# A Strassen-like projection on one Trainium2 core: smaller leading input chunks, a later place for the sums of squares, and a new order of pair one's products

## The chip, the cores and the metric

The kernel runs on one core of one Trainium2 chip. The time is device microseconds of one execution; runs of a kernel are repeated and their median is given. TensorE (PE) does the matrix products, VectorE (DVE) and ScalarE (ACT) the elementwise work, GpSimd (POOL) almost nothing, and SyncE (SP) issues nearly all DMA transfers. Each engine runs its own instructions in its own order and waits on semaphores for the others.

## What is computed

One layer of a decoder trunk for 1024 prompt tokens and 8 x 4 sample tokens, with the same weights, all in float32. Cut to what matters:

```python
h    = x * rsqrt(mean(x*x, -1) + EPS) * norm_g          # 1056 tokens x 1024
proj = h @ w_in                                          # 1024 -> 3072
b, c, u, z_a, v, z_b = split(proj)                       # six parts of 512
cu   = c * u
y_a  = b * conv3(cu) * silu(z_a)                         # three taps, causal
pooled = window_mean(v) - v                              # windows 2, 4, 8, 16 by channel group
y_b  = (pooled @ pool_w) * pool_scale * silu(z_b)
out  = rmsnorm(x + concat(y_a, y_b) @ w_out) * final_g
```

The last rows of `cu` and of `v` are returned as new states.

## The kernel before

**Precision and layout.** Channels lie on the 128 partitions and tokens along the free dimension. The 1056 tokens are three column groups n0, n1, n2 of 352. Each float32 operand is split into a high part in the matrix unit's reduced float32 (ACT writes it) and a low part, the rest (DVE writes it); `split2` does both. A product is the sum of three passes, high x low, low x high and high x high. A block of one weight tile, 128 x 512 of weights against 512 x 352 of x, is 12 matmuls (`block`, line 238).

**The first projection.** The norm gain multiplies x while it is split (`split_x`); the row scale 1/rms is applied later, to the products. The first pair of output tiles (v and z_b of group 0) is computed plainly by `project_first` (line 196), while the input arrives: for each of eight row tiles k of x, in the column groups n2 and n0, and then n1. The input comes in four leading chunks (`GROUPS`, line 109), in rows k = 0, then 1 and 2, then 3 and 4, then 5 to 7. A chunk is three loads on SP's queue: its part of the weights (`wfraw`) and its part of the columns n2 and n0 (`raw`). `prep_w0` and `split_x` split what has landed. The two loads of n1 follow.

**The other eleven pairs.** Each pair of output tiles (`PAIRS`) uses a scheme with fewer products: n0 and n1 and the two halves of the 1024 channels form a 2 x 2 block matrix of x, multiplied with the pair's 2 x 2 weight blocks in seven products; n2 is done plainly (`plain`, `plain1`: `l` and `r`, in pair one `lr`). The sums of x blocks are S1 to S4, the sums of weight blocks T1 to T4. A pair's weights are loaded as `wraw`, their differences are formed by `make_t` in `tw` (three DVE operations), and `make_unit` splits them into four units: a (B11, B21), b (B12, B22), c (T1, T3), d (T2, T4). Products add up in three PSUM banks a, b, c: B11 opens bank a, which is copied to s1 and then takes B21; bank b takes T2 and is read with s1 into t1, takes T3 and is read into t2, takes T4; bank c takes T1, is read with t2, takes B22. A bank must be read before the next product goes into it, since the partial sum is what is wanted.

**Pair one** is written out by hand (lines 536 to 588), since S1 to S4 are formed during it: S1f to S4f are float32 sums in the buffers of `raw`, and S1 and S4 overwrite `raw[1]` and `raw[0]`. From line 489 to 588 PE, ACT, DVE and POOL keep the order of the program (`manual_schedule`); from line 641 on only PE does, and the scheduler places the other engines' work, and may place work of both sections between one another. SP's queue is placed by the scheduler too. The PE order of pair one before is `lr0`, a: B11, `lr1`, a: B21, b: T2, c: T1, b: T3, b: T4, c: B22.

**The row scales** need the sums of squares of all tokens. Tokens 0 to 639 come by rows (`load_rows` of `xres`, `square_rows` on ACT with an accumulated sum): rows 0, 1 and 2 lie in the buffers of R, R2 and `up`, rows 3 and 4 in `x34`, a weight slot. The other tokens come from `raw` (`squares_head`, `squares_last`), are added on DVE into `acc` (`sums_last`, `sums_head`), and eight matmuls with one column each (`sums_rest`, line 285, tile `rest`) add over the partitions. `rows` turns all sums into 1/rms and builds a diagonal matrix of it (`diag`); `rows_out` spreads it by matmuls (`pr`) into R and then squares it into R2. In pair two these are the hooks `rest` and `rows`.

**Afterwards** the gates, the convolution and the pooling are done beside the products of later pairs, and the output projection (lines 684 and 756) ends the kernel.

Of the kernel before, what the change touches and what calls it, by code (L numbers as in the profile page):

```python
# [7 lines left out]
F32 = mybir.dt.float32  # L8
# [5 lines left out]
P = 128  # L14
D = 1024
# [47 lines left out]
def trunk(ctx, tc, xt, xres, xct, w_first, w_in, w_out, pool_w, par, fg, sconv, spool,  # L63
# [20 lines left out]
    def snap(name):  # L84
        return sp.tile([P, TN], F32, tag="snap", name=name)

    def bank(name):
        return ps.tile([P, 512], F32, tag="ps", name=name)
# [17 lines left out]
        nc.sync.dma_start(raw[n][:, k:k + m, :], xt[:, n * KD + k:n * KD + k + m, :])  # L106


    GROUPS = ((0, 1), (1, 2), (3, 2), (5, 3))
    for k, m in GROUPS:  # L110
        nc.sync.dma_start(wfraw[:, k:k + m, :], w_first[:, k:k + m, :])
        for n in (2, 0):
# [118 lines left out]
    def block(pt, p, w, x, first, last):  # L231

        u, i = WHERE[w]
        t = unit[p, u]
        seq = [(k, a, b) for k in range(KH) for a, b in ((0, 1), (1, 0))]
        seq += [(k, 0, 0) for k in range(KH)]
        for s, (k, a, b) in enumerate(seq):
            nc.tensor.matmul(pt, t[:, a, i, k * P:(k + 1) * P], x[:, b, k],  # L238
                             start=first and s == 0, stop=last and s == len(seq) - 1,
                             skip_group_check=True)  # L240
# [174 lines left out]

    def strassen(p, S1, S2, S3, S4, hooks):
        (q, j), (_, _) = PAIRS[p]
        if q == "v":  # L420
            left = vb[:, PM:]
            right = szb[j] = tmp(f"szb_{j}")
            scale = R
        elif q == "c":
            left, right = tmp(f"t_{j}"), tmp(f"um_{j}")
            scale = R2
        else:
            left, right = tmp(f"z_{j}"), tmp(f"y_{j}")
            scale = R

        def plain(i, name):
            pt = bank(name)[:, :TN]
            block(pt, p, ("B11", "B12")[i], pl[0], True, False)
            block(pt, p, ("B21", "B22")[i], pl[1], False, True)
            return pt

        a = bank(f"a_{p}")[:, :TN]
        s1 = snap(f"s1_{p}")
        block(a, p, "B11", A11, True, False)
        nc.scalar.copy(s1, a)  # L440
        b = bank(f"b_{p}")[:, :TN]
        block(b, p, "T2", S2, True, False)
        t1 = snap(f"t1_{p}")
        vt(t1, b, s1, op=ADD)
        c = bank(f"c_{p}")[:, :TN]
        block(c, p, "T1", S1, True, False)
        hooks.get("rest", lambda: None)()
        pL = plain(0, f"l_{p}")
        hooks.get("rows", lambda: None)()
        vt(left[:, n2], pL, scale[:, n2], op=MUL)  # L450
        block(a, p, "B21", A12, False, True)
        vt(left[:, n0], a, scale[:, n0], op=MUL)
        block(b, p, "T3", S3, False, False)
        t2 = snap(f"t2_{p}")
        vt(t2, b, s1, op=ADD)
        vt(right[:, n1], c, t2, op=ADD)
        hooks["early"]()
        pR = plain(1, f"r_{p}")
        if q == "v":
            vt(right[:, n2], pR, R[:, n2], op=MUL)  # L460
        elif q == "c":
            vt(up[:, 2 + 2 * TN:], pR, left[:, n2], op=MUL)
        else:
            nc.scalar.copy(right[:, n2], pR)
        hooks["middle"]()
        block(b, p, "T4", A22, False, True)
        vt(left[:, n1], b, s1, op=ADD)
        vt(left[:, n1], left[:, n1], scale[:, n1], op=MUL)
        block(c, p, "B22", S4, False, True)
        vt(right[:, n0], c, t1, op=ADD)  # L470
        hooks["late"]()

        if q == "v":
            after_v(j)
            vt(right[:, both], right[:, both], R[:, both], op=MUL)
            silu(right)
        elif q == "c":
            vt(up[:, 2:2 + 2 * TN], right[:, both], left[:, both], op=MUL)
            after_u(j)
        else:  # L480
            silu(left)
            vt(left, left, keep["yc"], op=MUL)
            vt(right, right, left, op=MUL)
            finish_mix(right, f"a_{j}")
# [4 lines left out]
    with tc.manual_schedule(engines={ET.PE, ET.Activation, ET.DVE, ET.Pool}):  # L489
        for k0, m in GROUPS:  # L490
            prep_w0(k0, m)
            for k in range(k0, k0 + m):
                for n in (2, 0):
                    split_x(n, k, wfraw[:, k, 2 * P:])
                    project_first(n, k)
        nc.vector.tensor_copy(gain.rearrange("p (k o) -> p k o", o=1), wfraw[:, :, 2 * P:])
        gk = [gain[:, k:k + 1] for k in range(KD)]
        load_w(1)
        nc.sync.dma_start(part, par)
        xk = [load_rows(t, q[:, :D]) for t, q in enumerate((R, R2, up[:, 2:]))]  # L500
        slot[1] = {"a": 2, "b": 3, "d": 4, "c": 0}
        slot[2] = {"a": 1, "d": 2, "c": 0, "b": 4, "spare": 3}
        acc = tmp("acc")
        for k in range(KD):
            split_x(1, k, gk[k])
            project_first(1, k)
        sh = squares_head(acc)

        S3f, S2f, S1f = raw[1][:, :KH], raw[1][:, KH:], raw[0][:, :KH]
        vt(S3f, raw[0][:, :KH], raw[1][:, :KH], op=SUB)  # L510
        make_unit(1, "a")
        for k in range(KH):
            nc.scalar.activation(S3f[:, k], S3f[:, k], AF.Copy, scale=gk[k])
        for k in range(KH):
            nc.vector.scalar_tensor_tensor(S2f[:, k], S2f[:, k], gk[KH + k], S3f[:, k], op0=MUL, op1=SUB)
        make_t(1)
        make_unit(1, "b")
        for i in range(2):
            nc.scalar.copy(heads[i][:, n2], pm[i, 2])
        sq = squares_last()  # L520
        make_unit(1, "d")
        S2 = xtile("xa", "S2")
        split(S2, S2f)
        S3 = xtile("xb", "S3")
        split(S3, S3f)
        make_unit(1, "c")
        x34 = wtile(1, [P, 2, D], "x34", F32)
        xk += [load_rows(t, x34[:, t - 3]) for t in (3, 4)]
        load_w(2)
        for k in range(KH):  # L530
            nc.vector.scalar_tensor_tensor(S1f[:, k], S1f[:, k], gk[k], S2f[:, k], op0=MUL, op1=ADD)
        for t in (3, 4, 2):
            square_rows(t, xk[t])


        t_0, um = tmp("t_0"), up[:, 2:]

        def plain1(i):
            pt = bank(f"lr{i}_1")[:, :TN]
            block(pt, 1, ("B11", "B12")[i], pl[0], True, False)  # L540
            block(pt, 1, ("B21", "B22")[i], pl[1], False, True)
            return pt

        pL = plain1(0)
        pa, pb, pc = (bank(f"{q}_1")[:, :TN] for q in "abc")
        s1, t1, t2 = (snap(f"{q}_1") for q in ("s1", "t1", "t2"))
        block(pa, 1, "B11", A11, True, False)
        nc.scalar.copy(s1, pa)
        pR = plain1(1)
        block(pa, 1, "B21", A12, False, True)  # L550
        S4f = [tp.tile([P, 2, TN], F32, tag="tmp", name=f"S4f_{h}") for h in range(2)]
        for k in range(KH):
            nc.vector.scalar_tensor_tensor(S4f[k // 2][:, k % 2], raw[0][:, KH + k], gk[KH + k], S2f[:, k],
                                           op0=MUL, op1=SUB)
        S1 = xtile("xc", "S1")
        split(S1, S1f)
        make_unit(2, "a")
        for n in (0, 1):
            for i in range(2):
                nc.scalar.copy(heads[i][:, cols[n]], pm[i, n])  # L560
        block(pb, 1, "T2", S2, True, False)
        vt(t1, pb, s1, op=ADD)
        S4 = xtile("xd", "S4")
        for h in range(2):
            ks = slice(2 * h, 2 * h + 2)
            split2(S4[:, 0, ks], S4[:, 1, ks], S4f[h])
        block(pc, 1, "T1", S1, True, False)
        nc.scalar.copy(t_0[:, n2], pL)
        make_t(2, (0,))
        nc.scalar.copy(t_0[:, n0], pa)  # L570
        block(pb, 1, "T3", S3, False, False)
        vt(t2, pb, s1, op=ADD)
        vt(um[:, n1], pc, t2, op=ADD)
        make_t(2, (1,))
        make_unit(2, "d")
        for t in range(2):
            square_rows(t, xk[t])
        block(pb, 1, "T4", A22, False, True)
        vt(t_0[:, n1], pb, s1, op=ADD)
        make_unit(2, "c")  # L580
        block(pc, 1, "B22", S4, False, True)
        vt(um[:, n0], pc, t1, op=ADD)
        for _ in sums_last(acc, sq):
            pass
        sums_head(acc, sh)
        make_unit(2, "b")
        vt(up[:, 2 + 2 * TN:], pR, t_0[:, n2], op=MUL)
        vt(up[:, 2:2 + 2 * TN], um[:, both], t_0[:, both], op=MUL)
# [267 lines left out]
```

## Time and profile before

| | us |
|---|---|
| median of 3 runs (lowest, highest) | 380.45 (379.07, 380.75) |
| the profiled execution | 380.98 |
| its span, from the first to the last instruction | 379.2 |
| PE busy in the span | 367.1 |
| DVE busy | 278.8 |
| ACT busy | 147.0 |

The mean granted TensorE clock of the span is 0.982. Times in rows of the profile are from the start of the span; L238 is line 238 of the kernel. A row of the timeline begins with start and duration, names the engine, the line, the operation, what is written and read and its shape, and ends with the idle time before it and what ended that idle time. A row of the waits has who waited for whom, the total, the number of times and the longest.

### The profile page before, as it was taken

Reading aid. Unit: us, or ns where it says so; the run is one execution under the profiler, and the core shown is the slowest. Engines: PE = TensorE matmul, PEld = TensorE weight load, DVE = VectorE, ACT = ScalarE, POOL = GpSimd, SP = SyncE. Lnnn points to the kernel's source line nnn. Section 1 sums busy time; section 2 is a strip of 40 time slices with the busy share of each in tenths; the row PEclk is TensorE's granted clock in tenths of the full one; section 3 lists DMA queues with packets and bytes.
Section 4 is the critical chain, followed back from the end, with each engine's and each line's share of the span. In section 5 each row is a group of like instructions: output and inputs, shape, how many; then the busy total and the mean of one; then the engine's idle time right before and its main releaser. Section 6 shows DMA issues by size and latency. Waiting matters only on the chain.

```text
span 379.2 us, 5200 instructions
## 1 busy us (share of the span) xinstructions
PE 367.1 (97%) x2114; PEld 353.4 (93%) x2114; DVE 278.8 (74%) x433; ACT 147.0 (39%) x231; POOL 1.4 (0%) x7
## 2 busy tenths in 40 slices
PE   6999997999999999999999999999999999999993
PEld 3999996999999999999999999999998889999883
DVE  3899869799999986769797666969269628222593
ACT  4899751863323323133332322332069215111212
POOL 0000000000000000000000000000000000000000
PEclk9899997899999999999999999999999999999998
DMA  7975002111131310303040130404639923100042
GB/s 226 394 258 190 34 0 67 73 33 80 57 112 58 112 57 19 150 2 111 0 169 0 54 137 11 165 3 129 270 110 349 417 89 124 45 0 2 0 180 111
DMA packets 13079, 41.67 MB, mean 110 GB/s; under 512 B 3712, under 2 KB 4224, under 8 KB 11648
## 3 DMA queue, kind: packets, MB, share of 16 engines
q1 hardware_dynamic: 12912, 41.02, 29.2%
q8 instruction: 16, 0.26, 0.3%
q10 hardware_dynamic: 144, 0.33, 0.2%
q14 instruction: 7, 0.06, 0.0%
HBM read 32.92 MB, written 8.42 MB: 109 GB/s over the span
## 4 chain that ended last, share of the span: by engine, by line
PE 93%; DVE 3%; DMA 2%; ACT 1%; SPq 0%; issue 0%; DVEq 0%
PE b L238 16%; PE po L686 15%; PE l L238 11%; PE a L238 11%; PE c L238 10%; PE r L238 10%; PE pc L756 10%; PE pm L196 6%; PE lr L238 2%; PE pp L392 2%; DMA raw<-in_xt_dram 2%; ACT R L249 1%; PE rest L285 0%; DVE wc L158 0%; DVE sq L274 0%; ACT wd L157 0%
## 5 line engine op out<-in xcount | busy, mean ns | idle before, releaser
L686 PE MATMUL po<-wo,mix 128*128 128x512 f32 (+1 forms) x264 | 56.5, 374 | 0.0
L686 PEld LDWEIGHTS po<-wo,mix 128*128 128x128 f32 x264 | 46.3, 188 | 9.7 <-DVE mix L158 0.2
L238 PE MATMUL a<-A,wa 128*128 128x352 f32 x264 | 46.4, 324 | 0.0
L238 PEld LDWEIGHTS a<-A,wa 128*128 128x128 f32 x264 | 43.3, 188 | 0.0
L238 PE MATMUL l<-pl,wa 128*128 128x352 f32 x240 | 42.5, 335 | 0.0
L238 PEld LDWEIGHTS l<-pl,wa 128*128 128x128 f32 x240 | 41.0, 197 | 0.0
L238 PE MATMUL r<-pl,wb 128*128 128x352 f32 x240 | 40.4, 324 | 0.0
L238 PEld LDWEIGHTS r<-pl,wb 128*128 128x128 f32 x240 | 39.1, 188 | 0.0
L756 PE MATMUL pc<-mix,wo 128*128 128x416 f32 x192 | 36.5, 351 | 0.0
L756 PEld LDWEIGHTS pc<-mix,wo 128*128 128x128 f32 x192 | 35.9, 188 | 0.5
L238 PE MATMUL c<-S,wc 128*128 128x352 f32 x132 | 23.4, 324 | 0.0
L238 PE MATMUL c<-S,wb 128*128 128x352 f32 x132 | 23.1, 324 | 0.0
L238 PE MATMUL b<-S,wc 128*128 128x352 f32 x132 | 23.1, 324 | 0.0
L238 PE MATMUL b<-S,wd 128*128 128x352 f32 x132 | 23.1, 324 | 0.0
L238 PE MATMUL b<-A,wd 128*128 128x352 f32 x132 | 23.1, 324 | 0.0
L157 ACT ACTIVATE wd<-tw 128x1024 fp32r<-128x1024 f32 x11 | 11.7, 1062 | 28.4 <-PE a L238 20.7
L238 PEld LDWEIGHTS c<-S,wc 128*128 128x128 f32 x132 | 21.6, 188 | 0.3 <-DVE wc L158 0.3
L238 PEld LDWEIGHTS b<-S,wc 128*128 128x128 f32 x132 | 21.7, 188 | 0.0
L238 PEld LDWEIGHTS c<-S,wb 128*128 128x128 f32 x132 | 21.7, 188 | 0.0
L238 PEld LDWEIGHTS b<-S,wd 128*128 128x128 f32 x132 | 21.7, 188 | 0.0
L238 PEld LDWEIGHTS b<-A,wd 128*128 128x128 f32 x132 | 21.7, 188 | 0.0
L758 DVE TENSOR_TENSOR zc<-pc,zc 128x416 f32<-128x416 f32 x8 | 4.7, 591 | 18.6 <-PE pc L756 18.6
(198 smaller groups left out, 530.7 us busy)
## 6 DMA issues: line engine op xcount, KB each, us to landing
wraw<-in_w_in_dram SPq DMA_DIRECT2D x11, 1024.0 KB, 4.7
woraw<-in_w_out_dram SPq DMA_DIRECT2D x8, 512.0 KB, 5.6
zt<-in_xres_dram SPq DMA_DIRECT2D x5, 512.0 KB, 6.2
spill_b<-yb SPq DMA_DIRECT2D x4, 528.0 KB, 2.8
mixraw<-spill_b SPq DMA_DIRECT2D x4, 528.0 KB, 6.4
out_yt_dram<-zt SPq DMA_DIRECT2D x4, 512.0 KB, 2.6
zc<-in_xct_dram SPq DMA_DIRECT2D x4, 416.0 KB, 7.2
out_yc_dram<-zc SPq DMA_DIRECT2D x4, 416.0 KB, 2.4
```

The source lines that it names most:

```text
L157: nc.scalar.activation(hi, src, AF.Copy)
L196: nc.tensor.matmul(pm[i, n], w0[k // KH][:, a, k % KH, i * P:(i + 1) * P], blocks[n, k // KH][:, b, k % KH], start=k == 0 and s == 0, stop ...
L238: nc.tensor.matmul(pt, t[:, a, i, k * P:(k + 1) * P], x[:, b, k], start=first and s == 0, stop=last and s == len(seq) - 1, skip_group_chec ...
L249: nc.scalar.activation(xk, xk, AF.Square, accum_out=ss[:, t:t + 1])
L392: nc.tensor.matmul(pt[:, :TN], pws[:, a, g, :], pooled[g][b][:, cols[n]], start=(s == 0), stop=(s == 2))
L686: nc.tensor.matmul(pt, mix[k][:, b, t * P:(t + 1) * P], wo[k][:, a, c], start=(k == 0 and s == 0), stop=(k == KD - 1 and s == 2))
L756: nc.tensor.matmul(pt, wo[k][:, a, d * P:(d + 1) * P], mix[k][:, b, T0:], start=(k == 0 and s == 0), stop=(k == KD - 1 and s == 2))
L758: nc.vector.tensor_tensor(zc[d], pt, zc[d], op=ALU.add)
```

## The change

- `GROUPS` becomes five chunks: rows 0, 1 and 2 alone, then 3 and 4, then 5 to 7. That is three loads more.
- After the first projection ACT copies both n2 and n0 of the first pair's products out of their banks; n1 is copied after S1's split, as part of what was copied there.
- The buffer `x34` is gone. Rows 3 and 4 of x are loaded into the buffers of rows 0 and 1 after those have been squared. Rows 2, 0, 1 are squared behind the copy s1 of pair one; rows 3 and 4 where 0 and 1 were.
- Unit a of pair two is made before S1f, in the slot that `x34` and then this unit used; before, it was made after S1's split.
- In pair one, T2 and its addition t1 stand before S4f and the splits of S1 and S4. The opening product of pair two (`first_a`: B11 into bank a, copied to s1) follows them, then T3, then T1, T4 and B22. `make_t(2)` is done in one piece ahead of t2; unit d of pair two stands between t2 and the addition into `um`.
- s1, t1 and t2 of pair one are slices of `t_0` and `um` in place of tiles of their own.
- In pair two, `rest` stands behind the plain product `l`, where it stood ahead of it. `rows` stands in the middle of the plain product `r`, where it stood behind `l`; the scaling of `l` and of bank a follows `r`.

The diff, shortened:

```diff
-    GROUPS = ((0, 1), (1, 2), (3, 2), (5, 3))
+    GROUPS = ((0, 1), (1, 1), (2, 1), (3, 2), (5, 3))
...
+    def first_a(p):
+        a = bank(f"a_{p}")[:, :TN]
+        s1 = snap(f"s1_{p}")
+        block(a, p, "B11", A11, True, False)
+        nc.scalar.copy(s1, a)
+        begun[p] = a, s1
...
-        def plain(i, name):
+        def plain(i, name, hook=None):
             pt = bank(name)[:, :TN]
             block(pt, p, ("B11", "B12")[i], pl[0], True, False)
+            if hook:
+                hook()
             block(pt, p, ("B21", "B22")[i], pl[1], False, True)
             return pt
...
+        pL = plain(0, f"l_{p}")
         hooks.get("rest", lambda: None)()
-        pL = plain(0, f"l_{p}")
-        hooks.get("rows", lambda: None)()
-        vt(left[:, n2], pL, scale[:, n2], op=MUL)
+        def scaled():
+            vt(left[:, n2], pL, scale[:, n2], op=MUL)
+            vt(left[:, n0], a, scale[:, n0], op=MUL)
...
-        pR = plain(1, f"r_{p}")
+        pR = plain(1, f"r_{p}", hooks.get("rows"))
+        if "rows" in hooks:
+            scaled()
...
-        for i in range(2):
-            nc.scalar.copy(heads[i][:, n2], pm[i, 2])
+        for n in (2, 0):
+            for i in range(2):
+                nc.scalar.copy(heads[i][:, cols[n]], pm[i, n])
...
         make_unit(1, "c")
-        x34 = wtile(1, [P, 2, D], "x34", F32)
-        xk += [load_rows(t, x34[:, t - 3]) for t in (3, 4)]
         load_w(2)
+        make_unit(2, "a")
         for k in range(KH):
             nc.vector.scalar_tensor_tensor(S1f[:, k], S1f[:, k], gk[k], S2f[:, k], op0=MUL, op1=ADD)
-        for t in (3, 4, 2):
-            square_rows(t, xk[t])
...
-        s1, t1, t2 = (snap(f"{q}_1") for q in ("s1", "t1", "t2"))
+        s1, t1, t2 = t_0[:, n1], um[:, n0], um[:, n1]
         block(pa, 1, "B11", A11, True, False)
         nc.scalar.copy(s1, pa)
+        for t in (2, 0, 1):
+            square_rows(t, xk[t])
+        xk += [load_rows(t, xk[t - 3]) for t in (3, 4)]
         pR = plain1(1)
         block(pa, 1, "B21", A12, False, True)
+        block(pb, 1, "T2", S2, True, False)
+        vt(t1, pb, s1, op=ADD)
         S4f = [...]
         ...
         split(S1, S1f)
-        make_unit(2, "a")
-        for n in (0, 1):
-            for i in range(2):
-                nc.scalar.copy(heads[i][:, cols[n]], pm[i, n])
-        block(pb, 1, "T2", S2, True, False)
-        vt(t1, pb, s1, op=ADD)
+        for i in range(2):
+            nc.scalar.copy(heads[i][:, n1], pm[i, 1])
         S4 = xtile("xd", "S4")
         ...
-        block(pc, 1, "T1", S1, True, False)
+        first_a(2)
         nc.scalar.copy(t_0[:, n2], pL)
-        make_t(2, (0,))
+        make_t(2)
         nc.scalar.copy(t_0[:, n0], pa)
         block(pb, 1, "T3", S3, False, False)
         vt(t2, pb, s1, op=ADD)
+        make_unit(2, "d")
+        block(pc, 1, "T1", S1, True, False)
         vt(um[:, n1], pc, t2, op=ADD)
-        make_t(2, (1,))
-        make_unit(2, "d")
-        for t in range(2):
+        for t in (3, 4):
             square_rows(t, xk[t])
         block(pb, 1, "T4", A22, False, True)
```

More of the change, by code (lines that the diff above doesn't have):

```diff
@@ L414, in after_u @@
         keep["yc"] = yc
+    begun = {}
+    def first_a(p):
[4 more added lines that the diff above has]
+        begun[p] = a, s1
     def strassen(p, S1, S2, S3, S4, hooks):
@@ L429, in strassen @@
             scale = R
-        def plain(i, name):
+        def plain(i, name, hook=None):
             pt = bank(name)[:, :TN]
             block(pt, p, ("B11", "B12")[i], pl[0], True, False)
+            if hook:
+                hook()
             block(pt, p, ("B21", "B22")[i], pl[1], False, True)
             return pt
[L437 to L440, printed above, removed]
+        if p not in begun:
+            first_a(p)
+        a, s1 = begun[p]
         b = bank(f"b_{p}")[:, :TN]
@@ L446, in strassen @@
         block(c, p, "T1", S1, True, False)
+        pL = plain(0, f"l_{p}")
         hooks.get("rest", lambda: None)()
-        pL = plain(0, f"l_{p}")
-        hooks.get("rows", lambda: None)()
-        vt(left[:, n2], pL, scale[:, n2], op=MUL)
+        def scaled():
+            vt(left[:, n2], pL, scale[:, n2], op=MUL)
+            vt(left[:, n0], a, scale[:, n0], op=MUL)
+        if "rows" not in hooks:
+            vt(left[:, n2], pL, scale[:, n2], op=MUL)
         block(a, p, "B21", A12, False, True)
-        vt(left[:, n0], a, scale[:, n0], op=MUL)
+        if "rows" not in hooks:
+            vt(left[:, n0], a, scale[:, n0], op=MUL)
         block(b, p, "T3", S3, False, False)
```

## The prediction

> **What bounds the kernel now.** I read the page's busy line and clock line first, then the waits of PE, then the windows cut at the clock's steps, then the chain of waits.
>
> ```profile
> PE 367.1 (97%) x2114; PEld 353.4 (93%) x2114; DVE 278.8 (74%) x433; ACT 147.0 (39%) x231; POOL 1.4 (0%) x7
> PEclk9899997899999999999999999999999999999998
> ```
> ```profile
> PE rest L285 <- DVE acc L262: 2.8, 1, 2.8
> PE pm L196 <- ACT pl L172: 2.5, 1, 2.5
> ```
> ```profile
> 3.44:6.85 3.41, 3.06 (x17) 2.10 (x14) 1.60 (x3) 1.39 (x3) 0.00 (x0) 1.00 0.85 225
> 6.85:10.26 3.41, 1.25 (x8) 1.25 (x9) 1.67 (x3) 2.23 (x5) 0.00 (x0) 1.00 1.03 386
> 10.26:13.67 3.41, 3.41 (x13) 3.41 (x13) 3.41 (x9) 3.41 (x9) 0.00 (x0) 0.50 1.04 423
> 58.05:61.46 3.41, 1.43 (x9) 1.14 (x8) 3.34 (x6) 0.00 (x0) 0.00 (x0) 1.00 0.00 0
> 61.46:64.87 3.41, 2.56 (x11) 2.53 (x12) 3.18 (x7) 0.33 (x3) 0.00 (x0) 0.50 0.17 31
> ```
> ```profile
> 9.01 23.08 PE pm L196 x132
> ...
> 43.73 1.94 PE b L238 x12
> ...
> 62.31 1.64 PE rest L285 x8
> 63.95 6.05 PE l L238 x24
> ```
>
> In a window row the first pair is its length and PE's busy time; after the five engines come the granted clock, the DMA share and GB/s. PE works 97% of the span, so only its pauses can be won. There are two before the tail, and each costs twice. The first, 2.5 us before 9.01, leaves 6.85:10.26 with 1.25 us of work (37%), and the next 3.41 us run at clock 0.50: 132 products take 23.08, where a block of 12 takes 1.94, so 132 would take 21.3. That pause is 2.5 + 1.7 us. The second runs from 62.31 - 2.83 = 59.48 to 62.31: PE waits for the sums of squares. Its window was busy for 1.43 of 3.41 us (42%), the next is at 0.50, and the 24 products behind need 6.05 instead of 3.88, until 70.00. That is 2.83 + 2.17 = 5.0 us.
>
> **The change, part by part.** The clock is the span's. E is the end of the first projection (line 196), now 9.01 + 23.08 = 32.09. Fixed PE work puts the end of pair one's T2 product at 45.67, E + 13.58, now and after.
>
> *Chunks 1, 1, 1, 2, 3.*
>
> ```profile
> 4.00 1.19 SPq L106 DMA_DIRECT2D raw<-in_xt_dram  x2
> ...
> 4.58 0.59 ACT L172 ACTIVATE A<-raw,wfraw 128x352 fp32r<-128x352 f32 x1 [0.32 <-DMA raw<-in_xt_dram]
> ...
> 7.48 0.63 ACT L157 ACTIVATE w<-wfraw 128x512 fp32r<-128x512 f32 x1 [2.32 <-DMA wfraw<-in_w_first_dram]
> 8.37 0.59 ACT L172 ACTIVATE pl<-raw,wfraw 128x352 fp32r<-128x352 f32 x1 [0.26 <-DMA raw<-in_xt_dram]
> ```
> ```profile
> 4.50:6.50 2.00, 2.00 (x12) 1.71 (x11) 0.97 (x2) 0.59 (x1) 0.00 (x0) 1.00 0.87 235
> ```
> ```profile
> raw<-in_xt_dram SPq DMA_DIRECT2D x4, 352.0 KB, 6.6
> ```
>
> Before row k=1 can be multiplied, its weights and x columns (304 KB) must land, where now it is two rows' (609 KB). Best: 304 KB at the 235 GB/s of 4.50:6.50, behind the landing at 4.58: 5.9, plus ACT's 0.59: 6.5, no pause at all. Worst: the transfers stall as now. Then 257 KB have landed at 7.48, the other 47 KB 0.1 us later, and PE starts at 8.25. The far end does not pay in full: the pair k=3, 4 comes no sooner, 6.6 us after its issue at 4.00, so about 10.6 to 11, split by 11.5, and 108 products follow it (17.5 us): E is 29.0 at the earliest. From the worst start E is 8.25 + 21.3 = 29.6. I take 29.5, nearest to the stalled rows, **-2.6 us**; 31.2 if the clock drops as now (-0.9), 32.1 if the landing does not move. Three more issues on SP stand before nothing PE is short of.
>
> *Squares' products behind pair two's plain product.*
>
> ```profile
> 57.74 1.25 DVE L274 TENSOR_TENSOR sq<-sq,sq 128x1056 f32<-128x1056 f32 x1
> ...
> 62.03 0.22 DVE L262 TENSOR_TENSOR acc<-sq_h 128x64 f32<-128x64 f32 x1
> ...
> 66.36 2.66 ACT L307 ACTIVATE diag<-ident,rh 128x128 fp32r<-128x128 f32 x9
> ```
>
> At 59.48 PE has 3.88 us of products that need no sums, so the pause and the half clock go: 10.52 us to 70.00 become 3.88 + 1.64, **-5.0**. Whether the sums are then there is worked out below. What is late next is the diagonal: it ends at 69.02, 5.1 us after `rest` (63.95), and PE has three blocks (5.8 us) before it asks: 0.7 us of cover.
>
>
> *Pair one's order.* This is where I see the price. T2 and the DVE addition behind it (t1) now stand ahead of S4f, S1, S4 and the weight differences of pair two (tw). DVE has been strictly in program order: it sat idle with ready work behind a blocked instruction (1.51 us before S1's low half, with the unit a of pair two to do; that unit runs after it, as written).
>
> ```profile
> 39.78 2.06 DVE L553 SCALAR_TENSOR_TENSOR S4f<-raw,gain,raw 128x352 f32<-128x352 f32 x4
> 41.94 1.38 ACT L157 ACTIVATE S<-raw 128x1408 fp32r<-128x1408 f32 x1 [2.47 <-DVE S4f L553]
> 43.35 1.62 DVE L158 TENSOR_TENSOR S<-raw,S 128x1408 fp32r<-128x1408 f32 x1 [1.51 <-ACT S L157]
> ...
> 45.54 1.50 ACT L157 ACTIVATE S<-S4f 128x704 fp32r<-128x704 f32 x2
> 46.03 0.52 DVE L562 TENSOR_TENSOR t<-b,s 128x352 f32<-128x352 f32 x1
> 46.47 1.69 DVE L158 TENSOR_TENSOR S<-S4f,S 128x704 fp32r<-128x704 f32 x2
> ...
> 48.07 1.22 DVE L213 TENSOR_TENSOR tw<-wraw 128x1024 f32<-128x1024 f32 x1
> 49.39 1.29 PE L238 MATMUL a<-A,wa 128*128 128x352 f32 x7
> 49.59 0.53 DVE L572 TENSOR_TENSOR t<-b,s 128x352 f32<-128x352 f32 x1 [0.30 <-PE b L238]
> ...
> 50.59 0.68 DVE L215 TENSOR_TENSOR tw<-wraw,tw 128x512 f32<-128x512 f32 x1
> 51.31 0.69 DVE L216 TENSOR_TENSOR tw<-wraw,tw 128x512 f32<-128x512 f32 x1
> 52.04 1.06 ACT L157 ACTIVATE wd<-tw 128x1024 fp32r<-128x1024 f32 x1 [4.30 <-DVE tw L216]
> ...
> 53.13 1.23 DVE L158 TENSOR_TENSOR wd<-tw,wd 128x1024 fp32r<-128x1024 f32 x1 [1.13 <-ACT wd L157]
> ```
>
> Now S4f and S1 are done (44.97) before T2 ends. After, DVE waits for T2's end; counted from there: t1 0.5, S4f 2.1 (2.6), S1's high half on ACT, which overwrites what S4f reads, 1.5 (4.1), its low half on DVE 1.6 (**5.7**): only now can T1 start. PE has the moved opening product and T3, 3.9 us: it **waits 1.8 us**. On DVE follow S4 (0.8 of ACT, then 1.69: 8.2), all of tw (2.6: 10.8) and then t2, 0.5 (11.3). T4 adds into the bank that t2 must read first, and PE has ended T1 at 7.6: it **waits 3.6 us**. Now t2 stands between the steps of tw, at 49.59, and seven products of the opening block (row 49.39) fill PE's wait; that cover is moved ahead of T3. PE idles 1.8, works 1.94 and idles 3.6, so wherever the windows of 3.41 us begin, one is at most some 46% busy, mostly far less: as after the two pauses above, one window of half clock, **+1.7**. It swallows a 0.4 us wait of B22, whose bank is read only behind wd (11.3, ACT 1.06, DVE 1.23 and 0.53: 13.6, where T4 ends at 13.2).
>
> The Trainium skill, "TensorE: Matmul & The Clock Gate" (Why this matters for your kernels), asks to avoid PE idle gaps over about 3 us, as one window of idle brings the half clock back. The trace is harder: 2.5 and 2.83 us sufficed. By the Trainium skill's measure only the 3.6 us wait is in danger, and by its "idle window" perhaps not even that.
>
> *Costed at nothing.*
>
> ```profile
> wraw<-in_w_in_dram SPq DMA_DIRECT2D x11, 1024.0 KB, 4.7
> ```
> ```profile
> 33.06 30.73 SPq L121 DMA_DIRECT2D wraw<-in_w_in_dram  x2
> 34.72 1.05 ACT L157 ACTIVATE wc<-tw 128x1024 fp32r<-128x1024 f32 x1
> ...
> 44.17 0.43 ACT L560 COPY vb<-pm 128x352 f32<-128x352 f32 x1
> ...
> 53.00 1.04 ACT L249 ACTIVATE R<-R 128x1024 f32<-128x1024 f32 x1
> ```
>
> Two head copies (0.4 each) come earlier on ACT and push pair one's units and S2, S3 back 0.8 us. They all stand ahead of unit c (34.72) there, and T2 asks first at E + 11.6 = 41.1: some five us of cover. Unit a of pair two moves ahead of S1f: its weights' load, without two x loads in front of it, is issued some 0.9 us before 33.06 and takes 4.7, so it lands at 36.8, just as ACT leaves unit c (34.72 + 1.05 + 0.8). Behind it on ACT stand the snapshot of the first block and three squares, and the snapshot is wanted at E + 9.7 = 39.2, over a microsecond later. On DVE it pushes the end of S1f from 39.78 to 41.7 (0.8, and 1.2 for the low half), before T2's end at 43.1. x rows 3 and 4 wait on SP for the squares of rows 0 and 1; behind them stands only a load that waits for unit b anyway. POOL's queue is not touched. Their squares (1.04 and a read, 1.1 each) stand before unit c of pair two as rows 0 and 1 did: wd's high half ends 11.9 after T2's end, the squares 14.1, c's halves 15.2 and 16.4; pair two asks for c three blocks after T4's start, at 17.1. Uncovered, it costs what it is late. The sums follow on DVE, an addition of 0.5 and then 57.74 to 62.25 as now: 21.4; PE asks for them after pair two's third block and the plain product, at 17.1 + 1.9 + 3.9 = 22.9. The three snaps become slices of buffers whose x rows have been squared by then.
>
> *Sum against the profiled execution* (380.98 us, span 379.2, 1.8 around it): -2.6 - 5.0 + 1.8 + 3.6 + 1.7 = **-0.5**, so 380.5. That execution lies 0.5 above the median of 380.45: **380.0 us**. All later work is the same PE stream, in the same order.
>
> **The rivals.**
>
> *Half-busy windows throttle too (slower).* Windows of 37 and 42% lost the clock, one of 90% (3.06 of 3.41) kept it; between them nothing is shown. From the stalled start at 8.25, 6.85:10.26 would be 59% busy; a window holding all of `rest` has 52% of wide products. If the gate drops from 60% down, both cost 1.7 us: 380.0 + 3.4 = 383.4. For it: 61.46:64.87 held 1.64 of `rest` and stayed at half speed. Against: a wait there too, and both windows depend on where boundaries fall.
>
> *Chunks bring nothing (slower, narrowly).* If landing is set by the first transfers' latency, E stays 32.1: 382.6. For it: 7.48 is 2.9 us behind 4.58 for 257 KB. Against: only these rows.
>
> *The new waits do not come (faster).* If t1 did not hold DVE, or later work filled PE there, the 1.8, 3.6 and 1.7 fall away: 372.9; with T1's wait left, 374.7. Against: the additions must read their banks between those products, and the next PE block needs wd, 13.1 from T2's end.
>
> *No half clock at the new waits (faster, just).* Two waits with a block between them might leave no window empty enough: without the 1.7, but with B22's 0.4, and a better landing (29.0), 378.2. The Trainium skill's rule above comes to this case.
>
> **How the numbers follow.** A measurement of this kernel can tell about 0.5% (1.9 us). Forecast 0.45: the landing's bounds (-3.1 to -0.9 for -2.6) give 379.5 to 381.7, with 0.8 either way for the spread of the runs 378.7 to 382.3; half-busy windows 0.17, chunks nothing 0.10, no waits 0.18, no half clock 0.10. Faster 0.28, same 0.45, slower 0.27. The range leaves out the case without waits (0.18): 376.5 to 383.6, with 1.7 below the fourth case for the spread of the runs.
>
> **What would show it.** Right: no wait of PE on `acc`; waits of PE on S1 (DVE line 158) near 1.8 and on t2 near 3.6; idle DVE before t1; clock 0.50 near 55, not at 10 and 62; `pm` ending near 29.5. Wrong: DVE working on S4f before T2 ends, PE blocks filling the two places, or `pr` waiting for the diagonal.

## The result, and the profile after

| | before | after |
|---|---|---|
| median (lowest, highest), 4 runs each | 380.6 (379.07, 380.91) | 384.66 (383.58, 385.08) |
| ratio after to before, 95% interval | | 1.0111 (1.0076 to 1.0145) |
| the profiled execution, its span | 380.98, 379.2 | 384.62, 382.8 |

The changed kernel is about 1.1% slower, 4.7 us above the forecast and 1.1 above the range. The waits of PE show at once how much of the forecast stands. A row names who waited for whom, then the total, the number of times and the longest.

```profile
PE b L238 <- DVE up L589: 3.4, 1, 3.4
PE c L238 <- DVE S L158: 2.2, 1, 2.2
PE b L238 <- DVE t L454: 2.0, 1, 2.0
PE pm L196 <- ACT pl L172: 1.1, 1, 1.1
```

The first is T4 of pair one behind t2 (forecast 3.6), the second T1 behind S1 (1.8), the fourth the first projection, whose pause was 2.5. The wait on `acc` is gone. The third row was in no sum and in no rival: a product of pair three, T3, waits 2.0 us for that pair's t1 (line 454).

PE's timeline after shows how far the forecast held, and where it broke. A row has start, duration, engine, line, what is written and read.

```profile
29.77 4.04 PE L238 MATMUL lr<-pl,wa 128*128 128x352 f32 x24
...
49.63 2.21 PE L238 MATMUL c<-S,wc 128*128 128x352 f32 x12 [2.23 <-DVE S L158]
55.20 3.37 PE L238 MATMUL b<-A,wd 128*128 128x352 f32 x12 [3.36 <-DVE up L589]
...
68.48 0.88 PE L285 MATMUL rest<-one,acc 128*128 128x1 f32 x8
...
75.21 1.12 PE L315 MATMUL pr<-diag,onesr 128*128 128x352 f32 x6
...
82.00 2.10 PE L238 MATMUL a<-A,wa 128*128 128x352 f32 x12
...
95.84 3.12 PE L238 MATMUL b<-S,wc 128*128 128x352 f32 x12 [2.04 <-DVE t L454]
```

The same products in the timeline before:

```profile
82.45 2.10 PE L238 MATMUL a<-A,wa 128*128 128x352 f32 x12
...
94.09 2.10 PE L238 MATMUL b<-S,wc 128*128 128x352 f32 x12
```

Up to the first block of pair three the change was worth 82.00 - 82.45 = -0.45 us, and the forecast's sum was -0.5 (how far that is luck is said below). Some twelve microseconds later T3 starts 95.84 - 94.09 = 1.75 us late, and its block takes 3.12 instead of 2.10. The windows after, cut at the clock's steps, show why (length and PE's busy time first; after the engines come clock, DMA share, GB/s):

```profile
45.60:49.01 3.41, 1.79 (x12) 1.50 (x10) 1.59 (x3) 2.07 (x3) 0.00 (x0) 1.00 0.01 2
49.01:52.43 3.42, 2.21 (x12) 1.92 (x12) 2.56 (x4) 2.52 (x5) 0.00 (x0) 1.00 0.00 0
52.43:55.84 3.41, 0.64 (x4) 0.64 (x5) 2.65 (x5) 1.10 (x2) 0.00 (x0) 1.00 0.00 0
55.84:59.25 3.41, 3.41 (x14) 3.41 (x12) 2.30 (x4) 3.41 (x6) 0.00 (x0) 0.50 0.00 0
...
93.39:96.80 3.41, 1.37 (x9) 1.08 (x8) 3.41 (x7) 1.08 (x1) 0.00 (x0) 1.00 0.00 0
96.80:100.21 3.41, 3.41 (x13) 3.41 (x12) 3.40 (x6) 0.33 (x2) 0.00 (x0) 0.50 0.38 159
```

The two waits of pair one cost one window of half clock, as forecast. The wait in pair three costs another. So the part not foreseen is 2.0 of wait and 1.7 of half clock, 3.7 us. The spans differ by 3.6, where -0.5 was forecast: 4.1 in all, of which 0.4 stay open.

What t1 of pair three waited for stands in the timeline of DVE and ACT after:

```profile
69.63 0.17 DVE L293 TENSOR_SCALAR mru<-ss 128x9 f32<-128x9 f32 x1 [1.38 <-ACT ss L287]
...
77.90 1.07 ACT L317 ACTIVATE R<-R 128x1056 f32<-128x1056 f32 x1
...
83.37 1.25 DVE L612 TENSOR_TENSOR up<-up,R 128x1056 f32<-128x1056 f32 x1
...
95.20 0.15 DVE L382 TENSOR_TENSOR pl<-first,vb 128x1 f32<-128x1 f32 x1
95.27 0.52 DVE L454 TENSOR_TENSOR t<-b,s 128x352 f32<-128x352 f32 x1
```

The rows at 83.37 and 95.20 are the first and the last of sixteen operations ahead of t1, and none of them has an idle time before it: DVE works from 83.37 to 95.27 without a gap, 11.90 us, nearly all of it `scale_heads` (the first heads multiplied by the row scale, convolution, pooling), and t1 stands in the queue behind it. `scale_heads` needs R and its square, these need `pr`, and `pr` needs `rest`. But R was not what came late: its square is written by 78.97 (the ACT row), 4.4 us before `scale_heads` starts. Late was the queue as a whole. DVE stood idle for the results of `rest` until 69.63, and of the 25.64 us from there to t1 it was busy for 24.84. Before, the same queue ran earlier:

```profile
78.03 1.25 DVE L595 TENSOR_TENSOR up<-up,R 128x1056 f32<-128x1056 f32 x1
...
92.37 0.52 DVE L444 TENSOR_TENSOR t<-b,s 128x352 f32<-128x352 f32 x1
```

There t1 ended 1.2 us before T3 asked at 94.09.

### The profile page after: what moved, and what is told of

Same layout as the page of the kernel before. It is cut to its first block, busy times and chain, and to the rows that moved or that the text cites. A ratio compares the mean times of both kernels' runs of the same rounds, so it can differ in the third digit from the quotient of the medians.

```text
span 382.8 us, 5206 instructions
## 1 busy us (share of the span) xinstructions
PE 367.1 (96%) x2114; PEld 352.4 (92%) x2114; DVE 279.1 (73%) x434; ACT 147.1 (38%) x232; POOL 1.4 (0%) x7
## 4 chain that ended last, share of the span: by engine, by line
PE 73%; DVE 3%; issue 1%; ACT 0%; DVEq 0%
PE po L703 15%; PE b L238 13%; PE pc L773 10%; PE r L238 9%; PE c L238 9%; PE l L238 8%; PE a L238 8%; PE pp L392 2%; DVE yc L409 0%; DVE yc L413 0%; DVE z L500 0%; DVE vb L614 0%; DVE up L612 0%; DVE win L370 0%; DVE pl L375 0%
## 5 line engine op out<-in xcount | busy, mean ns | idle before, releaser
L238 PE MATMUL r<-pl,wb 128*128 128x352 f32 x240 | 41.2, 327 | 0.0
L238 PE MATMUL l<-pl,wa 128*128 128x352 f32 x240 | 40.4, 324 | 0.0
L238 PEld LDWEIGHTS r<-pl,wb 128*128 128x128 f32 x240 | 39.9, 192 | 0.0
L238 PEld LDWEIGHTS l<-pl,wa 128*128 128x128 f32 x240 | 39.1, 188 | 0.0
L238 PE MATMUL b<-A,wd 128*128 128x352 f32 x132 | 24.4, 336 | 3.4 <-DVE up L589 3.4
L238 PE MATMUL b<-S,wc 128*128 128x352 f32 x132 | 24.1, 333 | 2.0 <-DVE t L454 2.0
L238 PEld LDWEIGHTS b<-A,wd 128*128 128x128 f32 x132 | 22.6, 196 | 3.7 <-DVE up L589 3.7
```

## The experiments

**Theory D**: DVE's queue sets the pace at two places. The first is S1 in pair one. The second is the chain `rest`, `diag`, `pr`, R, `scale_heads`, t1 of pair three. A pause of PE ahead of `rest` gives that chain time; where the pause goes, the chain has to be waited for. **Theory P**: each pause of PE has its own price, what is won at one is kept, and the wait in pair three comes from what pair one's new order leaves undone on DVE. In the diffs "before" and "after" are the two kernels; ratios are to the kernel before, on the same chip.

### The chunks alone (before, one line)

```diff
-    GROUPS = ((0, 1), (1, 2), (3, 2), (5, 3))
+    GROUPS = ((0, 1), (1, 1), (2, 1), (3, 2), (5, 3))
```

> The kernel before with the five leading chunks and nothing else. Theory D (VectorE's queue sets the pace): the first projection ends near 30 instead of 32.1, but S1 of pair one, unit c of pair two (57.4) and the sums (62.3) come from VectorE at the times of before, so PE waits at T1 (about 1.5 us) and longer for the sums (4 to 5 us in place of 2.8): 380.6 us within 0.7, no gain. Theory P (each pause of PE has its own price): what the start gains stays, 2.2 us: 378.4.

Measured: 381.11 us, ratio 1.0024 (1.0009 to 1.0039). PE's timeline:

```profile
29.37 4.04 PE L238 MATMUL lr<-pl,wa 128*128 128x352 f32 x24
...
45.30 2.19 PE L238 MATMUL c<-S,wc 128*128 128x352 f32 x12 [1.70 <-DVE S L158]
...
62.18 1.63 PE L285 MATMUL rest<-one,acc 128*128 128x1 f32 x8 [2.83 <-DVE acc L262]
```

The first projection ends 2.6 us sooner than in the profile before (31.93 there), and nothing of it arrives: T1 now waits 1.7 for S1, and `rest` stands at 62.18 where it stood at 62.31. D holds for the time, P doesn't. D's longer wait for the sums (4 to 5 us) did not come: it is 2.83 as before, since the waits of pair one had used up the earlier start.

### The later place of the sums alone (before, with the change's pair two)

```diff
         pL = plain(0, f"l_{p}")
+        hooks.get("rest", lambda: None)()
...
-        pR = plain(1, f"r_{p}")
+        pR = plain(1, f"r_{p}", hooks.get("rows"))
```

> The kernel before with only pair two's hooks changed: rest behind the plain product l, rows inside r, the scaling behind r. Theory D: VectorE needs about 26.4 us from the end of rest to the addition t1 of pair three, PE asks for it 24.4 us after rest; so PE waits about 2.0 us at T3 of pair three and loses a window of clock (1.7): of the 5.0 us, 1.7 us gain are left: 378.9 us. Theory P (the wait in pair three comes from VectorE's idle time in the new order of pair one, which is not in this kernel): no wait there, 375.6 us.

Measured: 379.33, ratio 0.9985 (0.9968 to 1.0002). PE's timeline and DVE's:

```profile
62.51 0.88 PE L285 MATMUL rest<-one,acc 128*128 128x1 f32 x8
...
90.73 3.73 PE L238 MATMUL b<-S,wc 128*128 128x352 f32 x12 [2.89 <-DVE t L446]
```
```profile
78.25 1.25 DVE L605 TENSOR_TENSOR up<-up,R 128x1056 f32<-128x1056 f32 x1
...
90.16 0.52 DVE L446 TENSOR_TENSOR t<-b,s 128x352 f32<-128x352 f32 x1
```

This is the plainest run of the study. The 2.83 us pause at `rest` is gone, and 28 us later there is one of 2.89 with a window of half clock behind it. Pair one has its old order here, so P's reason for that wait falls. From the first product with R to t1 are 90.16 - 78.25 = 11.91 us, as after (11.90).

### Old order of pair one (after, with T2, T1, `first_a` and the parts of `make_t` back in their old places)

```diff
-        block(pb, 1, "T2", S2, True, False)
...
         split(S1, S1f)
...
+        block(pb, 1, "T2", S2, True, False)
+        vt(t1, pb, s1, op=ADD)
```

> The changed kernel with pair one's order of before (S4f and the split of S1 ahead of T2's addition, T1 ahead of T3, the weight differences in two steps); chunks, moved sums and row buffers stay. Theory D: the waits at T1 and T4 shrink, but PE still waits for S1 (about 3 us, since PE comes early and VectorE does not), and T3 of pair three waits about 2 us again: 380 to 381 us. Theory P: 384.7 less 5.6 of waits, 1.7 of clock, 2.0 and 1.7 in pair three: 373.7 us.

Measured: 384.34, ratio 1.0108 (1.0087 to 1.0129). Both theories missed by over 3 us. DVE's timeline, with S1f and S4f between the two rows:

```profile
38.52 1.22 DVE L158 TENSOR_TENSOR wa<-wraw,wa 128x1024 fp32r<-128x1024 f32 x1
...
45.52 1.63 DVE L158 TENSOR_TENSOR S<-raw,S 128x1408 fp32r<-128x1408 f32 x1 [1.82 <-ACT S L157]
```
PE's waits in the same run:

```profile
PE c L238 <- DVE S L158: 4.3, 1, 4.3
PE b L238 <- DVE t L454: 2.9, 1, 2.9
```

Unit a of pair two (`wa`) still stands ahead of S1f, and S1 ends at 47.15, where it ended at 44.97. T1 waits 4.3 for it and two windows of half clock follow. The edit had left in place a part of the change that stands ahead of S1 on DVE. That this part holds up S1 is so far an inference; the run with unit a moved, below, tests it.

### Pair three's opening ahead of `scale_heads` (after, one part more)

```diff
             if p == 2:
+                first_a(3)
+                first_b(3, S2)
                 scale_heads()
```

`first_b` is T2 and its addition t1, taken out of pair three.

> The changed kernel with pair three's opening (B11, T2 and the addition t1) written ahead of the scaling of the first heads, so that t1 stands some eight VectorE operations earlier in its queue; no work is left out or added. Theory D: the wait at T3 of pair three and its half clock go (2.0 + 1.7): 381.0 us, and the wait does not come back at T4 of pair three (t2 ready about when PE asks). If the wait had another cause than that addition's place in the queue: 384.7 us as now.

Measured: 381.91, ratio 1.0046 (1.0028 to 1.0064), 2.75 us or, by the ratios, 0.65% below the kernel after. PE's waits, and t1 of pair three in DVE's timeline:

```profile
PE b L238 <- DVE up L598: 2.3, 1, 2.3
PE c L238 <- DVE S L158: 2.2, 1, 2.2
```
```profile
87.71 0.52 DVE L434 TENSOR_TENSOR t<-b,s 128x352 f32<-128x352 f32 x1
```

PE's order of products is that of after; t1 now runs at 87.71 and no longer behind all of `scale_heads`, and the wait in pair three is gone. So its place in the queue was the cause. The gain is 2.75 and not 3.7. In this profile the two waits of pair one cost three windows of half clock, where they cost one after, while T4's wait is 1.1 shorter.

### Later sums with that opening (before, with both), and the chunks with them

The edits are those of the second and the fourth experiment, made in the kernel before: its old chunks and its old pair one.

> The kernel before with the moved sums (as in e2) and pair three's opening ahead of the scaling of the heads (as in e4). Theory D, made sharper by e2 and e4 (behind the moved rest only the place of pair three's t1 in VectorE's queue takes the 5 us back): no wait at T3 of pair three, none at its T4 by a hair, about 4 us below before: 375.7 us. If VectorE's total work in that stretch binds wherever t1 stands, the wait comes back at t2 or at pair four, and it stays near e2, 379.3 us.

Measured: **375.94** (375.87 to 376.03), ratio **0.9881 (0.9852 to 0.9910)**. PE's waits:

```profile
PE c L238 <- DVE S L158: 1.0, 1, 1.0
PE pm L196 <- ACT pl L172: 0.8, 1, 0.8
...
PE b L238 <- DVE t L471: 0.7, 1, 0.7
```

This version is faster than both kernels, by 4.5 us against the one before (380.45 on that chip). That is nearly the term of -5.0 for the moved sums; it is won once t1 no longer waits. The third row, 0.7 at T4 of pair three, is what is left of DVE's queue there. No wait is longer than 1.0, and up to the tail the clock stays at 1.00.

The chunks of the first experiment were then added to it:

> e5 with the five leading chunks. Theory D: VectorE hands over S1 of pair one at 45 us whatever PE does, so the chunks bring nothing: within 0.7 us of e5, or a little more where the longer wait at T1 brings the half clock. Theory P: 2.2 us less than e5.

Measured: 377.13, ratio 0.9912 (0.9883 to 0.9940). T1 waits 1.7 for S1 instead of 1.0, and T4 of pair three 1.7 instead of 0.7. The median is 1.2 above that without the chunks, more than the 0.7 allowed for, though the two intervals overlap. The smaller chunks bring nothing here either.

### t2 of pair one ahead of `make_t(2)` (the fourth experiment, one line moved)

```diff
-        make_t(2)
         nc.scalar.copy(t_0[:, n0], pa)
         block(pb, 1, "T3", S3, False, False)
         vt(t2, pb, s1, op=ADD)
+        make_t(2)
```

> e4 with t2 of pair one ahead of the three weight-difference operations of pair two. The wait at T4 shrinks from 3.4 to about 0.9 us; unit d is not earlier, so about 1 us returns as a wait for it, and the stretch of low PE activity is broken: less half clock. Theory D: 1 to 2.5 us below e4 (381.9), 379.5 to 381. If the T4 wait were a cost by itself, 3.4 plus the half clock would go: 376.8 us.

Measured: 380.21, ratio 1.0006 (0.9987 to 1.0024), where the fourth experiment had 1.0046. PE's waits:

```profile
PE c L238 <- DVE S L158: 2.2, 1, 2.2
PE b L238 <- ACT wd L157: 1.5, 1, 1.5
PE b L238 <- DVE wd L158: 0.8, 1, 0.8
...
PE b L238 <- DVE up L597: 0.8, 1, 0.8
```

T4's wait falls from 2.3 to 0.8, and the weight differences, now behind t2, make unit d late: 1.5 + 0.8. The forecast's 3.6 was the time that DVE needs for S4 and `tw` ahead of t2. Turning the two round does not remove the waiting, it moves it to T2 of pair two: all waits behind the start of pair one were 4.5 us and are 5.3. What went down is the half clock, from three windows to one.

### `rest` back ahead of `l` (after, with only that undone)

```diff
+        hooks.get("rest", lambda: None)()
         pL = plain(0, f"l_{p}")
-        hooks.get("rest", lambda: None)()
+        hooks.get("rows", lambda: None)()
```

> The changed kernel with the sums' products ahead of the plain product l again and rows behind it, as before the change. Theory D: PE waits about 1.3 us for the sums, and the wait at T3 of pair three and its half clock go, because 3.9 us of PE work stand between rest and that addition again: 382 to 383 us, less than the changed kernel although a pause is put back. Theory P (the moved sums gain, the rest loses): slower than the changed kernel, 386 to 389 us.

Measured: 383.47, ratio 1.0079 (1.0049 to 1.0109). PE's timeline:

```profile
66.49 0.98 PE L285 MATMUL rest<-one,acc 128*128 128x1 f32 x8 [1.17 <-DVE acc L262]
```

PE waits 1.2 for the sums again, T3 of pair three no longer waits. The time is half a microsecond above D's range and well below P's. Within the changed kernel the moved sums thus won nothing (ratio 1.0111 with them, 1.0079 without, and the intervals overlap), where they were forecast to win 5.0. PE reached `rest` later because of pair one's waits, so most of the pause was gone anyway, and moving `rest` brought the wait in pair three.

### Old order with unit a behind S1, and the opening of pair three (the third and fourth experiments, one line more)

```diff
         load_w(2)
-        make_unit(2, "a")
...
         split(S1, S1f)
+        make_unit(2, "a")
```

> The kernel after with pair one's old order, unit a of pair two again behind S1's split, and pair three's opening (B11, T2, t1) ahead of the scaling of the first heads. If unit a ahead of S1f was what held S1 in the old order (S1's low half ended at 47.15 there, 44.97 in the kernel before), it ends near 45.5 to 46, T1 waits 2.0 to 3.0 in place of 4.3, the wait at T3 of pair three goes with its half clock (4.6), and the time is 384.34 - 4.6 - 1.3 to 2.3 = 377.5 to 378.5, with one half clock in pair one less 375.8 to 376.8. If S1 is held by the earlier copies of the first block or by the rows of x, T1 still waits 3.5 or more and the time is 379 to 381.

Measured: 378.89, ratio 0.9983 (0.9961 to 1.0004). DVE's timeline and PE's:

```profile
44.28 1.63 DVE L158 TENSOR_TENSOR S<-raw,S 128x1408 fp32r<-128x1408 f32 x1 [1.50 <-ACT S L157]
```
```profile
45.96 3.28 PE L238 MATMUL c<-S,wc 128*128 128x352 f32 x12 [2.80 <-DVE S L158]
49.04 2.60 PE L238 MATMUL b<-S,wc 128*128 128x352 f32 x12
```

S1 ends at 45.91, 1.24 before the third experiment: the duration of `wa` (1.22). T1's wait is 2.8, as expected. One window of half clock is left in pair one, where the third experiment had two, and for that case 375.8 to 376.8 was expected: the time is 2.1 above it. The window that went had been worth less than the 1.7 put down for it: it began at 45.97, so 1.2 of its 3.4 us were T1's wait, and 0.6 less was lost. T4 of pair three now waits 0.7. Together that is 1.3 of the 2.1; the rest stays open. What is settled is that unit a held S1; what keeps S1 another 0.9 us behind the kernel before (44.97) is not shown. And against the fourth experiment, which has this kernel's opening of pair three, the old order with the old place of unit a takes 0.6% off the ratio (1.0046 to 0.9983): the new order together with the new place of unit a costs more than it brings. With the new place kept, the order alone made no difference (1.0111 and, in the third experiment, 1.0108).

### The kernel before, profiled again

> The kernel before, unchanged, in another profiled execution. If the first pause of 2.5 us and its half clock belong to the chunks of two rows, PE waits 2.3 to 2.7 us for the second chunk again and pair one's lr starts at 31.5 to 32.3. If they belong to one execution's transfers, as 0.65 and 0.84 us with the same chunks in two other kernels suggest, the pause is anything from 0.5 to 2.5, lr starts at 29.4 to 32, and where the pause is short, T1 waits 1.0 us or more for S1, where it waited nothing. The time is 379 to 381 in either case.

Measured: 380.42, in one execution; whether on the chip of the first profile is not known. PE's timeline:

```profile
6.58 1.24 PE L196 MATMUL pm<-A,w 128*128 128x352 f32 x6 [1.05 <-ACT A L172]
8.28 1.25 PE L196 MATMUL pm<-pl,w 128*128 128x352 f32 x6 [0.47 <-ACT pl L172]
...
29.67 4.05 PE L238 MATMUL lr<-pl,wa 128*128 128x352 f32 x24
...
61.36 1.31 PE L285 MATMUL rest<-one,acc 128*128 128x1 f32 x8 [2.83 <-DVE acc L262]
```

The same kernel, the same chunks: the pauses are 1.05 and 0.47 instead of 2.51, no window of half clock follows them, and pair one starts at 29.67, where it started at 31.93. T1 waits 1.1 for S1 (in the first profile nothing), `rest` starts 0.95 sooner and the whole is 0.56 us shorter, of 2.26.

### All runs on one line each

Start of pair one (`lr`), PE's waits, and the windows of half clock ahead of the tail, from each run's profile; the time is the median (of one execution in the second row). The runs are on several chips, on which the median of the kernel before lay between 379.63 and 380.6; the ratios above are the better comparison.

| run | `lr` | T1 | other waits | windows | us |
|---|---|---|---|---|---|
| before (profiled first) | 31.93 | 0 | `rest` 2.8 | 3 | 380.6 |
| before again | 29.67 | 1.1 | `rest` 2.8 | 2 | 380.42 |
| after | 29.77 | 2.2 | T4 3.4, pair three 2.0 | 2 | 384.66 |
| chunks alone | 29.37 | 1.7 | `rest` 2.8 | 2 | 381.11 |
| later sums alone | 29.56 | 1.4 | pair three 2.9 | 1 | 379.33 |
| old order | 29.18 | 4.3 | pair three 2.9 | 3 | 384.34 |
| opening early | 29.70 | 2.2 | T4 2.3 | 3 | 381.91 |
| later sums, opening early | 29.93 | 1.0 | pair three 0.7 | 0 | 375.94 |
| the same with the chunks | 29.52 | 1.7 | pair three 1.7 | 0 | 377.13 |
| t2 ahead | 29.41 | 2.2 | T4 0.8, unit d 2.3 | 1 | 380.21 |
| `rest` back | 30.29 | 2.2 | T4 1.9, `rest` 1.2 | 3 | 383.47 |
| old order, unit a behind S1 | 29.42 | 2.8 | pair three 0.7 | 1 | 378.89 |

In each row `lr`, the waits and 1.7 per window behind `lr`, taken from that profile's span, leave 341.0 to 343.2. The waits and the clock explain the spread of nearly nine microseconds to within 2.2. A smaller loss of another kind could still hide in that.

## Why the prediction failed, point by point

**Sound by size.** T1's wait: 1.8 forecast, 2.2 found. T4's: 3.6 and 3.4. One window of half clock behind both, at 55.84. `rest` without a wait, and `pr` at 75.21 without a wait for the diagonal.

**Luck in the sum.** At 82.00 all this comes to -0.45, where -0.5 was forecast. That is as near as it is because misses cancel: the start brought 2.16 us and not 2.6, T1 cost 0.4 more and T4 0.2 less, and the moved sums brought 5.6 and not 5.0, mostly because `rest` at full clock takes 0.88 and not the 1.64 that the forecast kept. It also holds against one profile of before alone: in the other one the same block starts at 81.87, and after is then 0.13 us behind.

**The step that failed** is the last sentence of the sum: "All later work is the same PE stream, in the same order." PE's stream was the same; the work that feeds it was not, and later waits were put at nothing. What came was 2.04 us of wait at T3 of pair three and 1.7 of half clock. Moving `l` ahead of `rest` takes 3.88 us of PE's work from between `rest` and that T3, and full clock takes another 2.17 of duration there. What DVE must do between them stayed. The rows of before had most of the numbers. From the end of `rest` (63.95) to the end of t1 (92.89) DVE needed 28.9 us. Of these, 2.4 were work of pair two that could go ahead of `scale_heads` (from 78.03 to 92.37 are 14.3 us, after only 11.9; this the trace of before alone does not tell), which leaves 26.5. PE's own way from the end of `rest` to T3 (94.09) was 30.1 us, and without `l` (6.05) it is 24.1. That is a wait of about 2.4 us; it was 2.9 in the kernel with this part alone, and 2.0 after.

**"What is late next is the diagonal"** was a step too near. The diagonal came in time, and so did R. Late was the end of the queue that DVE takes up after `rest`, 27 us behind it.

**The chunks' -2.6** is a second step that failed, hidden by the first profile. In the trace the amount came (29.77 for 31.93), but the cause given for it did not hold. The kernel before reaches 29.67 with its own chunks in another execution, and alone the new chunks made the kernel 0.24% slower. The argument rested on one profile's landing times. Nor was the earlier start of use: with pair one as before, S1 ends at 44.35 to 44.97 in the four profiles with the old chunks, and at 45.16 and 45.32 in the two with the new ones. Why it ends later there is not shown.

**The rivals.** "Chunks bring nothing" was right about the chunks, though not by its reason: the first projection did end sooner. "Half-busy windows throttle too" did not come: windows of 52% and 65% (45.60:49.01 and 49.01:52.43 after) kept full clock. "No half clock at the new waits" and "The new waits do not come" did not come either. The time lies above that of every rival, since a wait in the next pair was in none.

## What to carry to other kernels

When a pause of PE is filled with later work, that work no longer covers what the pause's end starts: follow the chain from there, on every engine's queue, to the next place where PE asks for its end, and compare both lengths. Where a small operation that PE will ask for stands behind a long stretch on an in-order engine, put it ahead first; with that the same edit won 1.2% here, and without it 0.15%, which is not clear of zero. And before a pause of the start-up is counted as a gain, look at a second execution.

## What the runs showed of the hardware

**What costs the clock.** In the ten profiles with half clock ahead of the tail, the windows of 3.41 us on the clock's own grid can be sorted by PE's busy time without the one-column products of `rest`. Fifteen windows at full clock had 48% or less (the highest: 1.65 us in 55.00:58.41 of the run with t2 ahead), and all fifteen were followed by half clock. Twenty-seven had 52% to 90% (the lowest: 45.60:49.01 after; six of them were full and held `rest`), and none was. What counts is the sum in a window, not the length of one pause: T1's 2.23 us after, which lie in two windows, brought no half clock, and 1.17 us ahead of `rest` brought one in the run with `rest` back, whose windows read

```profile
64.08:67.49 3.41, 2.24 (x17) 1.92 (x15) 3.31 (x9) 0.00 (x0) 0.00 (x0) 1.00 0.00 0
67.49:70.91 3.42, 3.42 (x12) 3.42 (x13) 2.62 (x11) 1.01 (x6) 0.00 (x0) 0.50 0.69 232
```

Of the 2.24 us, 0.98 are `rest`; the other 1.26 are 37%. That one-column products do not count rests on this window alone among the fifteen; the others have 48% or less with them, too. The Trainium skill, "TensorE: Matmul & The Clock Gate" (Why this matters for your kernels), warns of idle gaps over about 3 us. By that, only T4's 3.4 after and the 4.3 of the old order were in danger; in these runs 2.0 us (pair three after) sufficed.

**What brings it back.** At half clock, windows that look busier did not restore it. In the run with the opening early:

```profile
50.35:53.76 3.41, 2.43 (x9) 1.98 (x7) 3.38 (x4) 1.69 (x4) 0.00 (x0) 0.50 0.00 0
53.76:57.17 3.41, 2.05 (x7) 2.06 (x8) 2.69 (x5) 2.51 (x4) 0.00 (x0) 0.50 0.00 0
57.17:60.59 3.42, 3.42 (x14) 3.42 (x13) 1.79 (x3) 2.63 (x4) 0.00 (x0) 0.50 0.00 0
```

The first two were 71% and 60% busy and half clock went on; the third was full, and full clock followed. In products of full clock the two did 1.2 and 1.0 us of work, under half a window; whether the gate counts work or time these runs do not settle. In the second profile of before, 61.76:65.17 was busy throughout, 0.91 us of it with `rest`, and half clock went on behind it. `rest` itself follows the clock: 1.64 us at half, 0.88 at full.

**How early transfers vary.** The pause behind the first chunk of two rows was 2.51 us in the first profile of before, and 0.65 in the kernel with the later sums alone, with the same chunks. Pair one starts 2.37 us sooner there, nearly the whole term that was argued from that pause.

**How the clock varies.** The kernel before was timed in 55 executions beside the experiments, on three chips. In 28 of them the mean granted clock was 0.990 to 0.995, and they took 378.80 to 379.71 us; in 27 it was 0.982 to 0.987, and they took 380.23 to 381.41. The 0.982 of the first profile came once in the 55. A window of half clock is 0.0045 of the mean, so one and the same kernel loses a different number of windows from one execution to the next, and a window seen in one profile is not a fixed price.
